# A gated-delta recurrence issued as a list of parts, with its product scalings on VectorE and its diagonal fills split over two engines

## The chip, the core and the metric

The kernel runs on one core of a Trainium2 chip. The metric is device time in microseconds (us) of one execution, lower is better. Five engines run their own instruction streams in order: TensorE (PE; its weight loads are shown as PEld), VectorE (DVE), ScalarE (ACT), GpSimd (POOL) and SyncE (SP, which issues the DMAs here). They wait for each other by semaphores.

## The reference, cut to what matters

One layer of a bidirectional backbone: a modulated norm, an input projection, two token mixers (a gated DeltaNet and a diagonal state-space model), gated merges, and a gated MLP with a 3x3 convolution. The change concerns the DeltaNet. Per head and direction, over chunks of tokens:

```python
lmat = jnp.where(strict, jnp.einsum('nbhcd,nbhsd->nbhcs', kb, k) * decay, 0.0)
sol = lax.linalg.triangular_solve(lmat, rhs, left_side=True, lower=True, unit_diagonal=True)
...
def step(state, xs):
    v_new = u_i - jnp.einsum('bhck,bhkv->bhcv', w_i, state)
    o = (jnp.einsum('bhck,bhkv->bhcv', q_i * jnp.exp(g_i)[..., None], state)
         + jnp.einsum('bhcs,bhsv->bhcv', a_i, v_new))
    state = (state * jnp.exp(g_last)[..., None]
             + jnp.einsum('bhck,bhcv->bhkv', k_i * jnp.exp(g_last - g_i)[..., None], v_new))
```

There are 4 heads of 128 columns and two directions; 1024 latent tokens follow 256 context tokens.

## The kernel before

The kernel works in chunks of 128 tokens: ten of them (two of context, eight of latents), taken forwards by direction 0 and in the mirrored order by direction 1. Step n handles one chunk of each direction, four heads at a time. Its work falls into these pieces:

- `delta_u` makes the decay matrix (the `gm` products of GpSimd, a matmul, an exponential on ScalarE, `affine_select` on GpSimd) and from it the triangular matrix `u` (VectorE, L928).
- `delta_pre` inverts it. The blocks of 32 on the diagonal are inverted in five levels (the **chain**): a matmul with `Ub` (L989), a copy by ScalarE into `Pe` (L992), a matmul with `Pe` (L995), a predicated copy and a transpose on VectorE (L974, L998). Then VectorE puts the diagonal blocks into the full matrices `Rf` and `Qf` (the **diagonal fills**, L1000 and L1001, four copies each), two rounds of corner products complete them, and a refinement step (`eh`, `el`, `dl`, `R2`; L1065 to L1086) makes the inverse `R2` exact enough. Chains of even and odd steps have their own tiles and PSUM bank (`la`, `lb`).
- `delta_step` is the recurrence: `ks` = keys times the state S (L1106); ScalarE scales it by row into `y` (L1108, four instructions); GpSimd adds `vtok` (L1109); `ty` = `R2` times y (L1113); VectorE multiplies by beta (L1115); `ds` (L1119); VectorE makes the new S (L1124). GpSimd prepares `kd` and `Sd`.
- `delta_out` makes the output: queries times S (L1138), scaled by ScalarE into `ob` (L1144, four instructions), queries times keys (L1147), and the product with y (L1152). `delta_post` norms a finished chunk.

The stage lies between the gate projections (`pz`, `pg`: plain large matmuls) and the gated linear unit (`gl`). `run` starts the chains of steps 0 and 1 ahead of the projections, so that they run beside them. The order on each engine is made by the framework's scheduler from the program's order in `delta`, one step after the other; the projections and the unit after the stage are ordered by it too. SP's queue holds the loads of `y_lo`, `w_raw` and `x` for what follows.

Of the kernel before, what the change touches and what calls it, by code (L numbers as in the profile page):

```python
# [7 lines left out]
F32 = mybir.dt.float32  # L8
# [14 lines left out]
NH = 4  # L23
# [22 lines left out]
class Zones:  # L46
# [6 lines left out]

DELTA_ZONES = {n: z for z, names in {
# [7 lines left out]
class Kernel:  # L62
    def __init__(self, tc, ins, out, stack):
        self.tc, self.nc, self.ins, self.out, self.es = tc, tc.nc, ins, out, stack
        self.dbg = {}
        self.flip = 0

# [825 lines left out]
    def delta_u(self, n, cs, tile, tag):  # L893
        nc, ps = self.nc, self.ps
        v, g_ = nc.vector, nc.gpsimd

        def b3(x):
            return x[:, :, None].to_broadcast([128, NH, 128])
# [4 lines left out]
        u = tile([128, 2 * NH, 128], F32, "u32", n)  # L903
        ats = []
        for r in range(2):
            c = cs[r]
            hs = slice(4 * r, 4 * r + 4)
            sp = bank()
            for i in range(2):
                gm = tile([128, NH, 128], F32R, "gm%d" % i, n)  # L910
                (g_).tensor_tensor(gm, (self.m_le, self.m_ge)[r][:, None, :].to_broadcast([128, NH, 128]),
                                 b3(r32(self.g_hl[i])[:, c, hs]), op=OP.mult)
                nc.tensor.matmul(sp.rearrange("p h i -> p (h i)"), lhsT=self.mr[r], rhs=gm.rearrange("p h i -> p (h i)"),
                                 start=(i == 0), stop=(i == 1))
            ei = tile([128, NH, 128], F32, "ei%d" % r, n)
# [3 lines left out]
            for out, cmp in ((es, OP.is_gt), (ei, OP.is_ge)):  # L919
                if cmp == OP.is_gt or c >= NCX:  # L920
                    g_.affine_select(out=out, in_=ei, pattern=[[0, NH], [sg, 128]], base=0, channel_multiplier=-sg,
                                     compare_op=cmp, fill=0.0)
# [7 lines left out]
            ats.append(ei)  # L930
        return u, ats

    def delta_pre(self, p, n, cs, given=None):
        nc, ps = self.nc, self.ps
        v, g_ = nc.vector, nc.gpsimd
        X = 2 * NH
        f3 = "p h i -> p (h i)"

        def m3(x, k=NH):
            return x[:, None, :].to_broadcast([128, k, 128])  # L940

        par = "ab"[n % 2]

        def bank(tag="pt"):
            return ps.tile([128, 512], F32, tag=tag, name="dps")

        lb = bank("l" + par)
        lvb = lb.rearrange("p (j x i) -> p j x i", j=2, x=X)

        def part(at, n):  # L950
            return lb[:, at:at + n * NH].rearrange("p (h i) -> p h i", h=NH)

        def grp(t):
            return t.rearrange("p (h i) -> p h i", h=NH)

# [741 lines left out]
```

## Time and profile before

| | |
|---|---|
| median of 3 runs | 1920.44 us (1917.15 to 1921.73) |
| the profiled execution | 1918.41 us |
| span of its trace | 1916.5 us |
| PE busy, share of the span | 1817.7 us, 95% |
| VectorE, ScalarE, GpSimd busy | 1346.1, 723.3, 815.9 us |
| mean granted TensorE clock | 0.975 |

The profile divides the span into 40 slices. PE shows 9 tenths or more in nearly all of them; apart from the start and the last slice only the 15th to the 19th, which are the recurrence, show 7 and 8, and the granted clock of TensorE is down to 0.8 in the 15th and 16th of them (the mark 9 stands for 0.9 or more). Busy shares say where an engine has room; what an instruction waited for is in the views of the waits and of the timeline.

### The profile page before, as it was taken

How to read it: one execution, taken by the hardware profiler on the slowest of the kernel's cores; microseconds unless marked ns; L12 is line 12 of the kernel's file. 1: busy time of each engine (PE TensorE's matmuls, PEld its weight loads, DVE VectorE, ACT ScalarE, POOL GpSimd, SP SyncE). 2: the span in 40 equal slices, each digit the busy share in tenths (PEclk: the TensorE clock that was granted, in tenths of full speed). 3: DMA queues.
4: the chain of work that ended last, by engine and by line, in shares of the span. 5: the costliest groups of instructions: out<-in, count | busy, mean ns of one | idle time of the engine just before them, and what ended most of it. 6: DMA issues, size and time to landing. Idle time of an engine off the chain costs nothing.

```text
span 1916.5 us, 27632 instructions
## 1 busy us (share of the span) xinstructions
PE 1817.7 (95%) x10874; PEld 1497.5 (78%) x10874; DVE 1346.1 (70%) x1922; ACT 723.3 (38%) x1457; POOL 815.9 (43%) x562
## 2 busy tenths in 40 slices
PE   8799999999999987888999999999999999999997
PEld 2488788787899966877778887788888888888886
DVE  8869999577666456766645245986777777767778
ACT  6423223345445466676632244322211221222222
POOL 3631322356445075554522343544425444443543
PEclk9899999999999988999999999999999999999999
DMA  8132333534414300001434332211111111111102
GB/s 337 40 91 79 90 104 89 160 103 133 143 42 117 95 2 2 2 2 45 158 127 139 110 88 72 61 55 43 46 44 55 45 47 52 46 44 43 56 22 88
DMA packets 186037, 149.27 MB, mean 78 GB/s; under 512 B 21426, under 2 KB 159282, under 8 KB 185908
## 3 DMA queue, kind: packets, MB, share of 16 engines
q1 hardware_dynamic: 184468, 142.27, 24.8%
q0 software_dynamic: 1440, 5.24, 0.7%
q8 instruction: 85, 1.39, 0.3%
q14 instruction: 44, 0.36, 0.1%
HBM read 125.99 MB, written 19.40 MB: 76 GB/s over the span
## 4 chain that ended last, share of the span: by engine, by line
PE 69%; DVE 9%; ACT 4%; DMA 3%; issue 2%; POOL 2%; SPq 0%; POOLq 0%; ACTq 0%; DVEq 0%
PE up_ps L213 25%; PE dn_ps L1438 12%; PE pw L213 5%; PE pab L213 4%; PE pj L213 3%; PE pj L430 3%; PE pz L213 2%; PE pg L213 2%; PE dps L1065 1%; DMA ada_w<-in_w_ada 1%; PE ty_ps L1113 1%; PE dps L925 1%; ACT Pe L992 1%; PE o_ps L1147 1%; PE o_ps L1152 1%
## 5 line engine op out<-in xcount | busy, mean ns | idle before, releaser
L1429 DVE SCALAR_TENSOR_TENSOR cacc<-up_ps,colC,cacc 128x945 f32<-128x945 f32 (+3 forms) x360 | 430.1, 1196 | 59.0 <-ACT cacc L1419 51.8
L205 POOL TENSOR_TENSOR w_lo<-w_raw,w_hi 128x1024 fp32r<-128x1024 f32 (+1 forms) x100 | 218.0, 2181 | 418.9 <-ACT w_hi L204 398.1
L213 PE MATMUL up_ps<-h_lo,w_hi 128*128 128x512 f32 x704 | 277.8, 395 | 0.0
L213 PE MATMUL up_ps<-h_hi,w_lo 128*128 128x512 f32 x704 | 277.8, 395 | 0.0
L213 PE MATMUL up_ps<-h_hi,w_hi 128*128 128x512 f32 x704 | 277.2, 395 | 0.5 <-DVE cacc L1429 0.5
L204 ACT CAST w_hi<-w_raw 128x1024 fp32r<-128x1024 f32 (+1 forms) x110 | 105.1, 956 | 363.5 <-PE up_ps L213 163.1
L1448 DVE TENSOR_TENSOR x<-dn_ps,x 128x512 f32<-128x512 f32 x160 | 109.5, 686 | 114.1 <-PE dn_ps L1438 113.0
L213 PEld LDWEIGHTS up_ps<-h_hi,w_hi 128*128 128x128 f32 x704 | 132.0, 188 | 31.7 <-issue 0.9
L213 PEld LDWEIGHTS up_ps<-h_hi,w_lo 128*128 128x128 f32 x704 | 132.3, 188 | 30.9
L213 PEld LDWEIGHTS up_ps<-h_lo,w_hi 128*128 128x128 f32 x704 | 132.3, 188 | 30.8
L413 POOL TENSOR_TENSOR w_lo<-w_raw,w_hi 128x1024 fp32r<-128x1024 f32 x20 | 62.5, 3125 | 187.5 <-ACT w_hi L412 186.0
L1438 PE MATMUL dn_ps<-wd_lo,g_hi 128*128 128x512 f32 x352 | 138.1, 392 | 0.0
L1438 PE MATMUL dn_ps<-wd_hi,g_lo 128*128 128x512 f32 x352 | 137.5, 391 | 0.0
L1438 PE MATMUL dn_ps<-wd_hi,g_hi 128*128 128x512 f32 x352 | 135.5, 392 | 0.1
L430 PE MATMUL pj<-hl_lo,w_hi 128*128 128x512 f32 x272 | 110.0, 405 | 4.0 <-DVE hl_lo L187 2.5
L430 PE MATMUL pj<-hl_hi,w_lo 128*128 128x512 f32 x272 | 108.8, 400 | 3.0 <-POOL w_lo L413 3.0
L430 PE MATMUL pj<-hl_hi,w_hi 128*128 128x512 f32 x272 | 108.8, 400 | 0.5 <-ACT hl_hi L184 0.5
L1252 POOL TENSOR_TENSOR g_lo<-cacc,g_hi 128x1024 fp32r<-128x1024 f32 (+1 forms) x23 | 53.3, 2318 | 92.7 <-ACT g_hi L1251 89.2
L213 PE MATMUL pj<-hl_hi,w_hi 128*128 128x512 f32 (+1 forms) x256 | 89.8, 351 | 0.0
L1482 ACT ACTIVATE cacc<-cacc 128x1024 f32<-128x1024 f32 x22 | 23.3, 1058 | 175.7 <-DVE cacc L1429 175.7
L213 PE MATMUL pj<-hl_lo,w_hi 128*128 128x512 f32 (+1 forms) x256 | 88.4, 345 | 0.0
L213 PE MATMUL pj<-hl_hi,w_lo 128*128 128x512 f32 (+1 forms) x256 | 88.2, 345 | 0.0
(522 smaller groups left out, 4422.0 us busy)
## 6 DMA issues: line engine op xcount, KB each, us to landing
w_raw<-in_w_in SPq DMA_DIRECT2D x46, 512.0 KB
w_raw<-in_w_up SPq DMA_DIRECT2D x44, 512.0 KB
ada_w<-in_w_ada SPq DMA_DIRECT2D x64, 256.0 KB
wd_raw<-in_w_down SPq DMA_DIRECT2D x22, 512.0 KB
wa<-in_w_ada SPq DMA_DIRECT2D x16, 512.0 KB
g_d<-gth SPq DMA_DIRECT2D x32, 256.0 KB
t<-g_d SPq DMA_DIRECT2D x32, 256.0 KB
w_raw<-in_w_o SPq DMA_DIRECT2D x16, 512.0 KB
```

The source lines that it names most:

```text
L204: self.rounded = nc.scalar.copy(hi[:, :kt, :m], raw[:, :kt, :m]).ins
L205: self.lowered = (eng or nc.gpsimd).tensor_sub(lo[:, :kt, :m], raw[:, :kt, :m], r32(hi[:, :kt, :m])).ins
L213: mm = nc.tensor.matmul(out, lhsT=w[a][:, k, :m], rhs=h[b][k][:, sl] if isinstance(h[b], list) else h[b][:, k, sl], start=(n == 0), stop=( ...
L413: nc.gpsimd.tensor_sub(w[1], raw, r32(w[0]))
L430: nc.tensor.matmul(ps[:, :width], lhsT=w[a][:, k], rhs=h[b][:, k, :width], start=(e == 0), stop=(e == 3 * KT - 1))
L925: nc.tensor.matmul(kp[:, h, :], lhsT=self.kT[c][:, h, :], rhs=self.kT[c][:, h, :], start=True, stop=True)
L992: nc.scalar.copy(pe[g, :, g], pp[g])
L1252: (eng or self.nc.gpsimd).tensor_sub(pair[1][sl], x, r32(pair[0][sl]))
L1429: tap[:] = [v.scalar_tensor_tensor(out=o, in0=ui[:, r0 + dy:r1 + dy, c0 + dx:c1 + dx], scalar=cw[:, t * NFT + ct:t * NFT + ct + 1], in1=o, ...
L1438: nc.tensor.matmul(out, lhsT=g[a][:, i * 128:(i + 1) * 128], rhs=w[b][:, h * 512:(h + 1) * 512], start=(first and n == 0), stop=(last and ...
L1448: v.tensor_add(x2, dn, x2)
L1482: nc.scalar.activation(ga, ga, AF.Silu)
```

## The change

A small planner (`Flow`) takes the stage's work as 15 parts (generators). Each part yields, ahead of every operation, the engine, an assumed duration, the buffers it takes and the events it needs. The planner issues the operation that could start first by its assumed clocks, corrected by a rank per part (`DELTA_RANK`, a table of numbers). The stage is issued under `manual_schedule`, so this list is the order on the engines, and no scheduler moves it. Parts are, for each direction: states, keys, refinements, outputs, posts; and for both: `gm`, `u`, `uh`/`ul`, and the chains of even and of odd steps. `delta_begin` issues, ahead of the projections' second half, the chains of steps 0 and 1 to their end and of step 2 up to the inverse of its diagonal blocks; the scheduler still places these.

Three operations change: `y` is one pass on VectorE out of PSUM (four instructions, scale and add together) in place of four on ScalarE and one on GpSimd; `ob` is one VectorE instruction in place of four on ScalarE; the `Qf` fills go to ScalarE, the `Rf` fills stay on VectorE. The refinement's `eh`, `el`, `dl` and its PSUM bank (`pt0`, `pt1`) become separate for the two directions.

```diff
+class Flow:
+    HOP = {"PE": 0.35, "DVE": 0.1, "ACT": 0.1, "POOL": 0.1}
+    BIAS = 0.3
...
+                base = max([p[2] + self.HOP[p[3]]] + [self.at[x] + 0.2 for x in chain(got, events)])
+                begin = [max(base, self.clock[e]) for e, _ in ops]
+                key = min(begin) + self.BIAS * p[0]
+                if best is None or key < best[0]:
+                    best = key, p, got, begin
...
+DELTA_RANK = (-27, 1.35, -2.3, 1.84, 2.03, 2.88, -39, 2.0, 2.57, 0.89, 2.85, -11.7, 1.85, 2.7, 1.89)
...
-            for h in range(NH):
-                nc.scalar.mul(y[:, h], kp[:, h], self.egn[:, c, 4 * r + h:4 * r + h + 1])
-            nc.gpsimd.tensor_add(y, y, self.vtok[c])
+                yield op("DVE", 1.37, (), old)
+                src = y = p.tile([128, NH, 128], F32, name="y%d" % r, bufs=2)
+                for h in range(NH):
+                    v.scalar_tensor_tensor(out=y[:, h], in0=kp[:, h], scalar=self.egn[:, c, 4 * r + h:4 * r + h + 1],
+                                           in1=self.vtok[c][:, h], op0=OP.mult, op1=OP.add)
...
-        for h in range(NH):
-            nc.scalar.mul(ob[:, h], oq[:, h], self.dec[:, 0, c, 4 * r + h:4 * r + h + 1])
+        v.tensor_mul(ob, oq, self.dec[:, 0, c, 4 * r:4 * r + 4, None].to_broadcast([128, NH, 128]))
...
-        for g in G:
-            v.tensor_copy(Rf[g, :, g], R[g])
-            v.tensor_copy(Qf[g, :, g], Q[g])
...
+        for g in G:
+            v.tensor_copy(Rf[g, :, g], R[g])
+            nc.scalar.copy(Qf[g, :, g], Q[g])
...
+        for n in range(2):
+            f.begin(self.uhl_part(p, n, self.pre[n]))
+            f.begin(self.chain_part(p, n, self.pre[n]))
+        f.free("u32")
+        f.run([(0, x) for x in self.u_two(p, 2, [o[2] for o in order])])
+        return f.begin(self.chain_part(p, 2, self.pre[2]), "inverse")
...
+            (rank[3], each(lambda n: begun if n == 2 else self.chain_part(p, n, pre[n]), ns[::2])),
+            (rank[4], each(lambda n: self.chain_part(p, n, pre[n]), ns[1::2])),
...
+                (rank[5 + 5 * r], self.state_part(p, r, order[r], pre)),
+                (rank[6 + 5 * r], self.keys_part(p, r, order[r])),
+                (rank[7 + 5 * r], each(lambda n, r=r: self.refine_part(p, n, r, pre[n]), range(NCH))),
+                (rank[8 + 5 * r], each(lambda n, r=r: self.out_part(p, n, r, cs[n][r], pre[n]), ns)),
...
+        with self.tc.manual_schedule():
+            self.flow.run(parts)
```

The order of the instructions shows what the list does. First VectorE, where the projections end and the first state product follows. Before (`Rf`, `Qf`: full matrices of a chain, `u`: the triangular matrix, here of step 2; `w_lo`: the projections' weights):

```order
L1001 COPY Qf_5812<-Qcb 32x8x32 x4
L205 TENSOR_TENSOR w_lo<-w_raw,w_hi 128x1024
L1029 CAST Rf_5588<-dps 32x4x32 x4
L205 TENSOR_TENSOR w_lo<-w_raw,w_hi 128x1024
L1052 CAST Rf_5588<-dps 64x4x64 x2
L1074 SCALAR_TENSOR_TENSOR el<-dps,eh 128x512 x2
L928 SCALAR_TENSOR_TENSOR u_6835<-dps,beta,es 128x128 x4
L1115 TENSOR_TENSOR y_6595<-ty_ps,beta 128x512
```

and now, at the same place (`Qca`, `Rca`: the even chain, here of step 2):

```order
L1196 CAST Rf_5941<-dps 64x4x64 x2
L1088 COPY_PREDICATED Rca<-lvl,dps 128x256
L1129 STREAM_TRANSPOSE Qca<-Rca 128x256
L1226 SCALAR_TENSOR_TENSOR el_6808<-dps,eh_6807 128x512
L1226 SCALAR_TENSOR_TENSOR el_6818<-dps,eh_6817 128x512
L1334 TENSOR_TENSOR ei_2_6039<-o_ps,ei_2_6039 128x512
L1088 COPY_PREDICATED Rca<-lvl,dps 128x256
L1129 STREAM_TRANSPOSE Qca<-Rca 128x256
L1334 TENSOR_TENSOR ei_2_6056<-o_ps,ei_2_6056 128x512
L1296 TENSOR_TENSOR y_6776<-ty_ps,beta 128x512
```

Step 2's `u` stood just ahead of the first state product, with its chain behind it; now two levels of that chain stand ahead of it, and the corner products of step 1 too.

Second VectorE in the middle of the stage. Before:

```order
L998 STREAM_TRANSPOSE Qca<-Rca 128x256
L1115 TENSOR_TENSOR y_7154<-ty_ps,beta 128x512
L1124 TENSOR_TENSOR S_7178<-ds_ps,Sd_7155 128x512
L1154 TENSOR_TENSOR o<-o_ps,ob 128x512
L928 SCALAR_TENSOR_TENSOR u_8089<-dps,beta,es 128x128 x4
L1115 TENSOR_TENSOR y_7182<-ty_ps,beta 128x512
L974 COPY_PREDICATED Rcb<-lvl,dps 128x256
L998 STREAM_TRANSPOSE Qcb<-Rcb 128x256
L1000 COPY Rf_5810<-Rcb 32x8x32 x4
L983 COPY Qcb<-eye 128x256
L1001 COPY Qf_5812<-Qcb 32x8x32 x4
```

and now (L1284 is the scaling into `y`, L1345 the one into `ob`):

```order
L1296 TENSOR_TENSOR y_7254<-ty_ps,beta 128x512
L1088 COPY_PREDICATED Rcb<-lvl,dps 128x256
L1129 STREAM_TRANSPOSE Qcb<-Rcb 128x256
L1284 SCALAR_TENSOR_TENSOR y_7313<-ks_ps,egn,vtok_3165 128x128 x4
L1345 TENSOR_TENSOR ob<-o_ps,dec 128x512
L1039 SCALAR_TENSOR_TENSOR u_7292<-dps,beta,es 128x128 x4
L1088 COPY_PREDICATED Rcb<-lvl,dps 128x256
L1129 STREAM_TRANSPOSE Qcb<-Rcb 128x256
L1353 TENSOR_TENSOR o<-o_ps,ob 128x512
L1311 TENSOR_TENSOR S_7388<-ds_ps,Sd_7216 128x512
L1296 TENSOR_TENSOR y_7313<-ty_ps,beta 128x512
```

The two scalings now stand between the chain's predicated copies, and the eight fills in a row are gone: four remain on VectorE per step.

Third SP, at the end of the stage. Before:

```order
L1268 DMA y_lo<-y_d 128x1024 x4
L200 DMA w_raw<-in_w_glu 128x4x128 x2
L1172 DMA sz_10317<-z_d 128x4x128
L1319 DMA t_10714<-g_d 128x512
L1319 DMA t_10715<-g_d 128x512
L1319 DMA t_10718<-g_d 128x512
L1319 DMA t_10719<-g_d 128x512
L200 DMA w_raw<-in_w_glu 128x4x128 x4
L1606 DMA x_11348<-in_x 128x1024 x3
L200 DMA w_raw<-in_w_glu 128x4x128
L1606 DMA x_11348<-in_x 128x1024 x5
L200 DMA w_raw<-in_w_glu 128x4x128
```

and now:

```order
L1372 DMA sz_10280<-z_d 128x4x128
L291 DMA w_raw<-in_w_glu 128x4x128 x2
L1563 DMA t_10677<-g_d 128x512
L1512 DMA y_lo<-y_d 128x1024 x4
L1563 DMA t_10678<-g_d 128x512
L1563 DMA t_10681<-g_d 128x512
L291 DMA w_raw<-in_w_glu 128x4x128
L1563 DMA t_10682<-g_d 128x512
L291 DMA w_raw<-in_w_glu 128x4x128 x3
L1846 DMA x_11311<-in_x 128x1024 x8
L291 DMA w_raw<-in_w_glu 128x4x128 x2
```

The loads of `y_lo`, with which the unit after the stage begins, moved behind two weight loads and one `t`; all eight loads of `x` moved ahead of that unit's last two weight loads.

## Rows read from the trace of the kernel before

**Rows 1.** Busy time of each engine by stretch, with granted clock (PEclk) and DMA.

```profile
core 0: us, PE busy (x) PEld busy (x) DVE busy (x) ACT busy (x) POOL busy (x), PEclk, DMA share, GB/s
570.00:668.00 98.00, 98.00 (x993) 95.74 (x991) 54.26 (x116) 51.39 (x120) 31.66 (x27) 1.00 0.36 103
668.00:922.00 254.00, 213.55 (x2665) 187.81 (x2663) 161.57 (x363) 173.04 (x485) 142.72 (x143) 0.91 0.06 19
668.00:768.00 100.00, 80.30 (x1004) 68.56 (x1003) 58.13 (x147) 68.59 (x178) 64.81 (x66) 0.86 0.01 3
768.00:922.00 154.00, 133.25 (x1663) 119.25 (x1662) 103.44 (x217) 104.45 (x307) 77.91 (x77) 0.93 0.09 29
828.00:888.00 60.00, 54.37 (x756) 48.97 (x755) 40.18 (x91) 48.79 (x153) 29.42 (x28) 0.97 0.04 11
```

**Rows 2.** Waits of PE, 668 to 924 us (total, times, longest).

```profile
PE ds_ps L1119 <- DVE y L1115: 6.0, 2, 3.7
PE dps L995 <- ACT Pe L992: 5.6, 5, 2.2
PE o_ps L1138 <- DVE o L1154: 4.8, 2, 4.5
PE dps L989 <- DVE Qca L998: 4.4, 2, 3.4
```

**Rows 3.** Groups of VectorE's instructions by shape, 668 to 922 us.

```profile
L928 DVE SCALAR_TENSOR_TENSOR u<-dps,beta,es 128x128 f32<-128x128 f32 x64 | 18.2, 342 | 6.5 <-PE dps L925 6.4
L1115 DVE TENSOR_TENSOR y<-ty_ps,beta 128x512 f32<-128x512 f32 x20 | 13.8, 691 | 16.6 <-PE ty_ps L1113 16.5
L1000 DVE COPY Rf<-Rcb 32x256 f16<-32x256 f16 x16 | 13.4, 835 | 0.2
...
L1001 DVE COPY Qf<-Qcb 32x256 f16<-32x256 f16 x16 | 7.1, 446 | 0.2
...
L1001 DVE COPY Qf<-Qca 32x256 f16<-32x256 f16 x16 | 5.2, 328 | 0.2
L1000 DVE COPY Rf<-Rca 32x256 f16<-32x256 f16 x16 | 3.5, 220 | 0.2
```

**Rows 4.** The same of ScalarE, 668 to 922 us.

```profile
L992 ACT CAST Pe<-dps 32x256 f16<-32x256 f32 x128 | 46.2, 361 | 9.9 <-PE dps L989 7.9
L1108 ACT ACTIVATE y<-ks_ps,egn 128x128 f32<-128x128 f32 x72 | 20.6, 370 | 12.9 <-PE ks_ps L1106 12.6
L1144 ACT ACTIVATE ob<-o_ps,dec 128x128 f32<-128x128 f32 x64 | 18.3, 376 | 10.8 <-PE o_ps L1138 10.8
```

**Rows 5.** The same of GpSimd, 668 to 922 us.

```profile
L1109 POOL TENSOR_TENSOR y<-y,vtok 128x512 f32<-128x512 f32 x18 | 23.0, 1276 | 14.2 <-ACT y L1108 14.1
```

**Rows 6.** Timeline of VectorE, 733 to 741 us (start, duration; x4 merged).

```profile
733.74 5.04 DVE L1000 COPY Rf<-Rcb 32x256 f16<-32x256 f16 x4
```

**Rows 7.** Timeline of GpSimd in the same 8 us.

```profile
733.57 2.14 POOL L965 TENSOR_TENSOR ul<-u,uh 128x1024 f16<-128x1024 f32 x1 [0.98 <-ACT uh L964]
735.66 1.04 POOL L911 TENSOR_TENSOR gm<-cm,dg_hi 128x512 fp32r<-128x512 f32 x1
...
737.66 1.04 POOL L1095 TENSOR_TENSOR kd<-ktok,dec 128x512 f32<-128x512 f32 x1
```

**Rows 8.** Timeline of VectorE, 760 to 922 us: first state product of steps 3 and 9.

```profile
767.08 0.69 DVE L1115 TENSOR_TENSOR y<-ty_ps,beta 128x512 f32<-128x512 f32 x1 [3.54 <-PE ty_ps L1113]
...
914.77 0.69 DVE L1115 TENSOR_TENSOR y<-ty_ps,beta 128x512 f32<-128x512 f32 x1 [2.20 <-PE ty_ps L1113]
```

**Rows 9.** Timeline of SP's queue, 640 to 960 us.

```profile
902.06 14.21 SPq L1268 DMA_DIRECT2D y_lo<-y_d  x4
...
953.79 0.38 SPq L200 DMA_DIRECT2D w_raw<-in_w_glu  x1
```

**Rows 10.** Timeline of ScalarE after the stage.

```profile
963.68 0.62 ACT L204 CAST w_hi<-w_raw 128x512 fp32r<-128x512 f32 x1 [4.01 <-DMA w_raw<-in_w_glu]
```

**Rows 11.** Timeline of PE after the stage.

```profile
924.15 0.50 PE L213 MATMUL gl<-y_hi,w_hi 128*128 128x512 f32 x1 [3.67 <-ACT w_hi L204]
```

More of the change, by code (lines that the diff above doesn't have):

```diff
@@ L54, with op @@
+def op(engine, us, takes=(), events=(), also=()):
+    return ((engine, us), *also), takes, events
+DELTA_RANK = (-27, 1.35, -2.3, 1.84, 2.03, 2.88, -39, 2.0, 2.57, 0.89, 2.85, -11.7, 1.85, 2.7, 1.89)
 DELTA_ZONES = {n: z for z, names in {
@@ L918, in delta_u, with keep @@
             sg = 1 if r == 0 else -1
[L919 to L922, printed above, removed]
+            def keep(out, cmp):
+                g_.affine_select(out=out, in_=ei, pattern=[[0, NH], [sg, 128]], base=0, channel_multiplier=-sg,
+                                 compare_op=cmp, fill=0.0)
+            yield op("POOL", 0.65, (), (), (("PE", 0.97),))
+            keep(es, OP.is_gt)
             kp = bank()
@@ L929, in delta_u, with delta_own @@
                                        op0=OP.mult, op1=OP.mult)
[L930 to L954, printed above, removed]
+            f.free("p1")
+            if c >= NCX:
+                yield op("POOL", 0.65)
+                keep(ei, OP.is_ge)
+            ats[r] = ei
+        f.fire("u%d" % n)
+    def delta_own(self, p):
         def own(shape, dt, name, n):
@@ L1047, in delta_pre @@
                 nc.tensor.matmul(r6[A, h, :], lhsT=P6[B, h, :], rhs=Rf[B, 4 * r + h, B], start=True, stop=True)
+        yield op("ACT", 0.76, also=(("DVE", 0.86),))
         for r in range(2):
@@ new lines, in refine_part @@
+        yield op("PE", 0.46)
+        d = bank()
+        for h in range(NH):
+            for k, t in enumerate((eh, el)):
+                mm(d[:, h, :], t[:, h, :], Rf[:, 4 * r + h, :], start=(h == 0 and k == 0))
+        yield op("ACT", 0.6)
+        nc.scalar.copy(dl, d)
+        yield op("PE", 0.44)
+        for h in range(NH):
+            mm(d[:, h, :], eh[:, h, :], dl[:, h, :])
+        mm(d.rearrange(f3), self.ident16, Rf[:, hs].rearrange(f3), stop=True)
+        yield op("ACT", 0.6, (), ("ty%d%d" % (n - 2, r),) if n >= 2 else ())
@@ L1171, in delta_post @@
             self.transpose(tp[:, h, :], o[:, h, :])
[L1172 removed]
+        yield op("DVE", 0.75)
         f = "p h t -> p (h t)"
@@ L1183, in delta @@
         order = self.delta_order()
[L1184 to L1204 removed]
+        pre = self.pre
@@ new lines, in delta, with each @@
+        ns = range(2, NCH)
+        cs = [[o[n] for o in order] for n in range(NCH)]
+        own = self.delta_own(p)
+        rank = DELTA_RANK
+        def each(part, over):
+            for n in over:
+                yield from part(n)
+        parts = [
+            (rank[0], each(lambda n: self.gm_part(n, cs[n], own), ns[1:])),
+            (rank[1], each(lambda n: self.u_part(p, n, cs[n], pre[n]), ns[1:])),
+            (rank[2], each(lambda n: self.uhl_part(p, n, pre[n]), ns)),
+            (rank[3], each(lambda n: begun if n == 2 else self.chain_part(p, n, pre[n]), ns[::2])),
+            (rank[4], each(lambda n: self.chain_part(p, n, pre[n]), ns[1::2])),
+        ]
@@ new lines, in delta @@
+        posts = [c - NCX for c in chain(*cs[NCH - 2:])]
+        for r in range(2):
+            parts += [
+                (rank[5 + 5 * r], self.state_part(p, r, order[r], pre)),
+                (rank[6 + 5 * r], self.keys_part(p, r, order[r])),
+                (rank[7 + 5 * r], each(lambda n, r=r: self.refine_part(p, n, r, pre[n]), range(NCH))),
+                (rank[8 + 5 * r], each(lambda n, r=r: self.out_part(p, n, r, cs[n][r], pre[n]), ns)),
+                (rank[9 + 5 * r], each(lambda n, r=r: self.post_part(p, cs[n][r] - NCX, z_d, ("out%d%d" % (n, r),)), ns[4:6])),
+            ]
```

404 lines of the change are left out of this document (285 added, 119 removed), and 2 rows, old and new, of the table DELTA_ZONES.

## The prediction

> **What bounds the kernel now.** I read the slices of the page first: PE is busy nearly everywhere, and only the recurrence has gaps. So I cut the middle of the span into stretches [rows 1]. From 570 to 668 us (projections, with the first chains beside them) PE is busy 98.00 of 98 us at clock 1.00: work put there makes it longer, microsecond for microsecond. From 668 to 922 us (the recurrence) PE is busy 213.55 of 254 us at a mean granted clock of 0.91. That clock is a mix of the two levels, 1.2 and 2.4 GHz, and at the lower one the same matmuls show as more busy time. So I take busy time times clock as the stage's PE work at full clock: 213.55 x 0.91 = 194 us. The **density** of the stage, work over time, is 194 / 254 = 0.77, and the 60 us that are not work (40.5 us of idle PE, some 19 us of lower clock) are all that an order can win. The first 100 us are worse, 0.803 x 0.86 = 0.69; the rest has 0.865 x 0.93 = 0.80; the best long stretch, 828 to 888 us, has 0.906 x 0.97 = 0.88.
>
> Next the waits of PE [rows 2]. No single one rules: 6.0 us for `ds` behind VectorE's y, 5.6 us behind ScalarE's `Pe`, 4.8 and 4.4 us behind VectorE. Each is a short dependence with too little other work queued between its two ends. VectorE, ScalarE and GpSimd are busy 161.57, 173.04 and 142.72 of 254 us [rows 1]: none is full, and each has stretches in which the others wait for it. One of these is plain: at 733.74 us four `Rf` fills take 5.04 us on VectorE [rows 6], where a fill takes 0.22 us in the undisturbed group [rows 3]. GpSimd runs without a gap meanwhile [rows 7], and its operations end at 735.7, 736.7, 737.7 and 738.7 us; four fills that wait for one of these ends each would be through at 738.8 us, as they are. `Qca`, which is made behind such fills in VectorE's queue, is what PE waits for up to 3.4 us [rows 2].
>
> **The change part by part.**
>
> *The state product's scaling.* 18 groups go from ScalarE (20.6 us, 72 instructions) [rows 4] and GpSimd (23.0 us) [rows 5] to VectorE. The nearest row for the new instruction is L928, the same operation on 128x128 with one operand in PSUM: 342 ns [rows 3]. So VectorE gains 72 x 0.342 = 24.6 us. On the path of one step ScalarE's four and GpSimd's one (4 x 0.370 + 1.276 = 2.8 us) become 4 x 0.342 = 1.4 us, one handover less. That is 1.4 us x 10 steps per direction, but the recurrence of one direction is not what fills the stage, so I count it in the density alone. These rows have 0.342 us on VectorE against 0.370 on ScalarE: no loss by the engine. The Trainium skill, Perfetto Trace Analysis, section Optimizing Scalar/DVE Operations, speaks against the move: it has a fixed cost per instruction of about 125 ns for VectorE on PSUM and about 51 ns for ScalarE. By that page the 72 instructions would be 72 x 0.074 = 5.3 us dearer, and the forecast, all of it exposed, 1893 us (an estimate from that page). The measured rows decide, and I leave it out.
>
> *The output's scaling.* 16 groups, 18.3 us off ScalarE [rows 4]; on VectorE one instruction each, of the form of L1115 (PSUM times a broadcast column): 16 x 0.691 = 11.1 us [rows 3].
>
> *The fills.* 32 `Qf` fills leave VectorE: 7.1 + 5.2 = 12.3 us [rows 3]. ScalarE has no such row; copies of that size out of PSUM, L992, take 361 ns [rows 4], so 32 x 0.361 = 11.6 us. It could be as little as the 0.22 us of VectorE's fill, 7 us; twice L992 would be 23 us. ScalarE, relieved of 38.9 us, hides either. The `Rf` fills stay: 16.9 us for 32 where 7.0 us would do, so about 10 us of stretching remain.
>
> Sum by engine, if the stage's work is the same: VectorE 161.6 + 24.6 + 11.1 - 12.3 = 185 us; ScalarE 173.0 - 38.9 + 11.6 = 146 us; GpSimd 142.7 - 23.0 = 120 us; PE unchanged. VectorE comes near to PE.
>
> *Work moved ahead.* Step 2's `u`, two levels of its chain and step 1's corner products now stand before the first state product, as VectorE's order shows. I bound what leaves the stage on PE by 3 to 8 us: the stage's 194 us are eight full steps, so 24 us each, and this is an eighth to a third of one. I take 5 us, and put them back on the projections, where PE has no room. They win nothing by themselves; what they win is the latency of a chain, which the first 100 us at 0.69 wait for.
>
> *The order.* This is the term that decides. The list has the two chains, both directions' states and the outputs side by side, and puts other work between the ends of the short dependences of [rows 2]; states run ahead where their inverses are ready. No row shows the new density. From below it is bounded by today's 0.77, unless a new wait comes (a rival); from above by 1.00. I take 0.87: today's order reaches 0.88 over its best 60 us [rows 1], with all pieces of the stage present, and the stage's last step, a serial chain with little left beside it, will not reach that. So the stage takes (194 - 5) / 0.87 = 217 us.
>
> *The end.* `y_lo` loads now stand behind two weight loads and one `t`, and `x` ahead of the last two weight loads. Today those loads wait on the stage's buffers for 14.21 us [rows 9], and PE idles 3.67 us ahead of the first `gl` [rows 11]; ScalarE waits 4.01 us for the last weights behind `x` [rows 10]. Bounds: 3.7 us won where the first gap goes, 9 us lost where both weights, and not only the last, come after all of `x` and twice the 4.01 us is exposed with an issue between. Queue places do not say which, so I take 0.
>
> *Small edits together.* Separate `eh`, `el`, `dl` for the directions, separate PSUM banks, other tags for the projections' `zth`: freer buffers, no instruction more; they are part of the order's term.
>
> **Sum.** 254 -> 217 + 5 = 222 us, 32 us less: 1918.4 - 32 = 1886 us against the profiled execution. The median of the runs shown is 2 us above that execution, which is inside the bounds, so I forecast **1886 us**.
>
> **The rivals.**
>
> 1. *Nearly full PE.* The list hides all but the last step's tail, density 0.95 or more: (189 / 0.95) + 5 = 204 us, 1868 us; at 1.00, 194 us, 1858 us. For it: 20 us at a stretch have run without a gap. Against: VectorE at 185 of 204 us would itself need to be nine tenths busy, in order, beside it.
>
> 2. *The chains keep the pace.* The first state product of step 3 comes at 767.08 us and that of step 9 at 914.77 us [rows 8]: 147.7 us for three more chains on each side, 49 us each. If a chain's handovers, each behind a queue, take as long as now, these 148 us stay, and only the start is won: the first 100 us at 0.69 go to 0.87, 69 / 0.87 = 79 us, less the 5 us moved and with them put back. That is 20 us at most and some 12 us where the start is only half mended: 1898 to 1906 us. For it: the chain's waits are among [rows 2]. Against: a list that puts the chain's matmuls earlier shortens its queues too.
>
> 3. *Given back.* The stage gets shorter by few us, and what it gets is lost at the end [rows 9 to 11]: 1915 to 1921 us. This also takes in the case that the assumed durations are wrong enough to make a fixed list no better than the scheduler's order.
>
> 4. *Slower: VectorE's queue holds PE.* VectorE gains 35.7 us and loses 12.3 us: 23.4 us more. The new scalings stand in its queue in front of the chain's predicated copies, and PE's chain matmuls wait for those. If the order wins nothing and every added microsecond is seen by PE, 1918.4 + 23.4 = 1942 us; at half, 1930 us. It decides from the point where VectorE, with its stretched fills, has no gap left in which to catch up, about nine tenths busy: today it has 161.57 of 254 us, then 185 of 222, 0.83, below that point. The same section of Perfetto Trace Analysis in the Trainium skill says that work belongs on ScalarE when VectorE is saturated; whether it is, its busy share in the new profile tells.
>
> That the change would not do what it says I exclude: the order shows the list's order on the engines, the scalings on VectorE and half the fills gone.
>
> **How the numbers follow.** What a measurement of this kernel can tell from no change is about 0.3%, 6 us. The forecast (density 0.83 to 0.94: 1900 to 1870 us) gets 0.56; nearly full PE 0.11; chains keep the pace 0.17; given back 0.07; slower 0.09. Faster is 0.56 + 0.11 + 0.17 = 0.84. The range of 8 in 10 reaches from 1862 us, inside the first rival, to 1910 us, past the second; outside lie the best third of rival 1 and rivals 3 and 4, 0.04 + 0.07 + 0.09 = 0.20.
>
> **What would show each step.** Right: the stretch from the last `pg` matmul to the first `gl` near 222 - 225 us, busy times clock over it near 0.87, and the gain largest in its first 100 us; VectorE near 185 us there, with the new `y` instructions at 0.34 us and `ob` at 0.69 us; ScalarE's `Qf` fills between 0.2 and 0.7 us; the projections some 5 us longer. The prediction is wrong if the waits of PE are led by one wait on VectorE of well over 10 us (rival 4), if steps 3 to 9 still take 148 us (rival 2), or if the gap ahead of `gl` grows by as much as the stage shrinks (rival 3).

## The result, and the profile after

The changed kernel takes 1886.48 us in the median of 4 runs (1885.86 to 1890.37) against 1920.72 us before: ratio 0.9833, 95% interval 0.9822 to 0.9845. That is faster by far more than the 0.3% that a measurement of this kernel can tell. The profiled execution took 1885.86 us, with a span of 1884.2 us. (In one experiment below, `a3`, the profiled execution was disturbed; its trace is not read, and its ratio is from its other runs.)

The stretches of the changed kernel, with the columns of [rows 1]; projections, the recurrence, its first 90 us, its rest, and the first 65 us of the projection behind it:

```profile
570.00:675.00 105.00, 103.52 (x1093) 100.48 (x1092) 60.39 (x124) 59.91 (x144) 34.29 (x31) 1.00 0.34 95
675.00:890.00 215.00, 191.70 (x2577) 171.37 (x2575) 169.15 (x402) 147.42 (x375) 118.21 (x120) 0.97 0.09 27
675.00:765.00 90.00, 76.79 (x998) 66.17 (x997) 64.29 (x159) 58.58 (x139) 52.45 (x54) 0.92 0.01 4
765.00:890.00 125.00, 114.91 (x1584) 105.20 (x1581) 104.86 (x245) 88.84 (x237) 65.77 (x66) 1.00 0.14 43
890.00:955.00 65.00, 64.62 (x272) 50.85 (x270) 35.09 (x38) 34.75 (x70) 26.30 (x22) 0.96 0.34 115
```

Work over time in the recurrence is 191.70 x 0.97 / 215 = 0.865, against 0.77 before [rows 1]. Of its parts the first 90 us have 0.785, the rest 0.92. Idle PE fell from 40.5 to 23.3 us; and as the granted clock rose from 0.91 to 0.97, busy time above the work at full clock fell from 19 to about 6 us. Of the 39 us by which the stretch got shorter (254 to 215 us), 17 are thus idle time, 13 are clock, and 8 are work that left it (194 to 186 us). ScalarE and GpSimd, 173 and 143 us before, have 147 and 118 us; VectorE has 169 us, 0.79 of the stretch.

To see where in the stage the time went, I use two landmarks that can be found in every kernel: the last `pg` matmul, where the projections end, and the state products on VectorE (`y<-ty_ps`, 20 of them). Here are the last `pg` group (a tile's view: counts, shortest/median/longest ns, first and last start), and the 7th and the 19th state product of the changed kernel (timeline of VectorE):

```profile
L304 PE MATMUL pg<-hl_hi,w_lo x96: 277/283/387, 634.0 to 674.5; 128*128 128x256 f32 x96
```

```profile
746.58 0.69 DVE L1296 TENSOR_TENSOR y<-ty_ps,beta 128x512 f32<-128x512 f32 x1 [0.44 <-PE ty_ps L1292]
...
879.31 0.68 DVE L1296 TENSOR_TENSOR y<-ty_ps,beta 128x512 f32<-128x512 f32 x1
```

(They are numbered by their start; in another order the same number can belong to another step, so small differences say little.) From the last `pg` to the 7th product ("start") it is 746.58 - 674.5 = 72.1 us, from the 7th to the 19th ("pace") 132.7 us. Before, the last `pg` started at 666.0 us and the same two products are those of [rows 8]: start 101.1 us, pace 147.7 us. So 29 us came from the start and 15 us from the pace. From the 19th product to the first `gl` it was 9.4 us and is 10.1 us. The whole balance: stage from last `pg` to first `gl` 258.16 to 214.93 us (-43.2), projections 94.0 to 101.0 us (+7.0), everything ahead of them +1.5, first `gl` to first `pab` (the output projections that follow) 49.5 to 50.3 us (+0.8), the rest +1.6; sum -32.3 us, which is the difference of the two spans, 1916.5 and 1884.2 us.

The waits of PE from 675 to 890 us (total, times, longest), to be read beside [rows 2]:

```profile
PE gl L304 <- ACT y_hi L1514: 4.7, 1, 4.7
PE dps L1124 <- ACT Pe L1120: 4.0, 5, 1.6
PE dps L1116 <- DVE Qcb L1129: 2.1, 1, 2.1
PE dps L1116 <- DVE Qca L1129: 1.9, 2, 1.5
```

The waits for `y` (6.0 us before, 0.4 us now) and for VectorE's `o` (4.8 us before, 0.7 us now) are no longer among the long ones. What is left is the chain of levels (`Pe`, `Qca`, `Qcb`), and one wait at the junction.

The groups that the change made or touched, VectorE and then ScalarE, 675 to 890 us, beside [rows 3, 4]:

```profile
L1284 DVE SCALAR_TENSOR_TENSOR y<-ks_ps,egn,vtok 128x128 f32<-128x128 f32 x72 | 19.9, 339 | 1.0 <-PE ks_ps L1280 1.0
...
L1345 DVE TENSOR_TENSOR ob<-o_ps,dec 128x512 f32<-128x512 f32 x16 | 10.9, 684 | 4.6 <-PE o_ps L1341 4.4
L1162 DVE COPY Rf<-Rca 32x256 f16<-32x256 f16 x16 | 7.2, 448 | 0.2
L1108 DVE COPY Qca<-eye 128x256 f16<-128x256 f16 x3 | 5.0, 1665 | 0.0
L1162 DVE COPY Rf<-Rcb 32x256 f16<-32x256 f16 x16 | 3.8, 237 | 0.2
L1108 DVE COPY Qcb<-eye 128x256 f16<-128x256 f16 x4 | 3.2, 801 | 0.0
```

```profile
L1120 ACT CAST Pe<-dps 32x256 f16<-32x256 f32 x124 | 44.9, 362 | 19.7 <-PE dps L1116 17.6
L1163 ACT COPY Qf<-Qca 32x256 f16<-32x256 f16 x16 | 6.4, 399 | 0.1
L1163 ACT COPY Qf<-Qcb 32x256 f16<-32x256 f16 x16 | 6.4, 398 | 0.1
```

(72 x 0.339 would be 24.4 us; the busy time of L1284 is 19.9 us, so neighbours overlap at their ends, and four take 1.1 us.)

### The profile page after: what moved, and what is told of

The parts are those of the page before. It is cut to its first block, busy times and chain, and to the rows that moved or that the text cites. A ratio compares the mean times of both kernels' runs of the same rounds, so it can differ in the third digit from the quotient of the medians.

```text
span 1884.2 us, 27551 instructions
## 1 busy us (share of the span) xinstructions
PE 1802.2 (96%) x10874; PEld 1488.5 (79%) x10874; DVE 1356.4 (72%) x1970; ACT 703.6 (37%) x1361; POOL 789.7 (42%) x542
## 4 chain that ended last, share of the span: by engine, by line
PE 54%; ACT 2%; DVE 2%; POOL 1%; issue 1%; POOLq 0%; ACTq 0%; DVEq 0%
PE up_ps L304 25%; PE dn_ps L1682 12%; PE pw L304 5%; PE pab L304 4%; PE gl L304 2%; PE dps L1211 1%; DVE cacc L1673 1%; PE o_ps L1341 1%; ACT Pe L1120 0%; PE o_ps L1349 0%; PE o_ps L1331 0%; PE dps L1035 0%; PE xn_ps L175 0%; PE ot_ps L175 0%; ACT fsq L1750 0%
## 5 line engine op out<-in xcount | busy, mean ns | idle before, releaser
L304 PEld LDWEIGHTS up_ps<-h_hi,w_hi 128*128 128x128 f32 x704 | 132.5, 189 | 31.7 <-issue 0.9
L304 PEld LDWEIGHTS up_ps<-h_lo,w_hi 128*128 128x128 f32 x704 | 132.7, 188 | 30.7
L1726 ACT ACTIVATE cacc<-cacc 128x1024 f32<-128x1024 f32 x22 | 23.3, 1058 | 175.7 <-DVE cacc L1673 175.7
```

The costliest lines, as they stand in the source:

```text
L304: mm = nc.tensor.matmul(out, lhsT=w[a][:, k, :m], rhs=h[b][k][:, sl] if isinstance(h[b], list) else h[b][:, k, sl], start=(n == 0), stop=( ...
L1726: nc.scalar.activation(ga, ga, AF.Silu)
```

## The experiments

The change is two things: the list, which fixes the order, and three engine moves (`y`, `ob`, `Qf` fills). My first theory was the prediction's: the order decides, and the moves give little. The first four runs try both apart. (The refinement's separate buffers and PSUM banks come with the list, and no run takes them away alone; `b2` below has them without the fixed order, and is no faster than the moves alone. Nor was `ob` undone alone.) Where I give what an edit costs against the changed kernel or another run, it is the difference of the two ratios times 1920 us; with their intervals it is good to some 4 us.

**Moves without the list** (`a1`): the kernel before, with only

```diff
-                nc.scalar.mul(y[:, h], kp[:, h], self.egn[...])
-            nc.gpsimd.tensor_add(y, y, self.vtok[c])
+                v.scalar_tensor_tensor(out=y[:, h], in0=kp[:, h], scalar=self.egn[...], in1=self.vtok[c][:, h], op0=OP.mult, op1=OP.add)
...
-            nc.scalar.mul(ob[:, h], oq[:, h], self.dec[...])
+        v.tensor_mul(ob, oq, self.dec[...].to_broadcast([128, NH, 128]))
...
-            v.tensor_copy(Qf[g, :, g], Q[g])
+            nc.scalar.copy(Qf[g, :, g], Q[g])
```

> The kernel before with the three engine moves alone: y as one VectorE operation per head, ob as one VectorE multiply, the first fills of Qf on ScalarE; the order is left to the scheduler as before. Theory (the list's order wins the time, by putting other work between the ends of the short dependences; the moves alone give little): 1908 to 1925 us, PE's density in the recurrence stage stays below 0.80 at full clock (before 0.77). Rival (the moves carry it: shorter chain around the state products, ScalarE and GpSimd relieved): 1885 to 1898 us, density at 0.83 or more.

Measured: 1900.14 us, ratio 0.9906 (0.9888 to 0.9925), some 18 us faster than before, between the two ranges. Its stage, from 667 to 907 us:

```profile
667.00:907.00 240.00, 211.80 (x2712) 185.68 (x2710) 175.76 (x420) 153.13 (x385) 123.11 (x126) 0.93 0.06 19
```

Density 211.80 x 0.93 / 240 = 0.82. So the moves alone are worth half of the gain: far more than my theory had. Its last `pg` starts at 669.0 us, its 7th and 19th state products at 758.85 and 898.25 us.

**The list without the moves, planned for the old operations** (`a2`): the changed kernel with the three edits above undone and the planner's durations to match, as here for `y`:

```diff
-                yield op("DVE", 1.37, (), old)
+                yield op("ACT", 1.48, (), old)
...
+                yield op("POOL", 1.28)
```

> The changed kernel with all three engine moves undone (y on ScalarE and GpSimd, ob on ScalarE, Qf fills on VectorE), the planner's durations set to match; the list stays. Theory (the list carries it): 1887 to 1900 us, two thirds of the gain of 34 us or more remains. Rival (the moves carry it): 1905 to 1921 us, two thirds or more of the gain is gone. In between, the two need each other.

Measured: 1923.57 us, ratio 1.0021 (1.0011 to 1.0031). All of the gain is gone; the time is even 2.6 us above the rival's range. The theory, that the list carries it, has fallen.

**One move undone at a time**, planned anew: `y` (`a3`) and the `Qf` fills (`a4`, planner's `also=(("DVE", 1.8),)`), with the same lines as above.

> The changed kernel with only y back on ScalarE and GpSimd (23 us of GpSimd and 20 of ScalarE for 20 of VectorE). Theory (other work lies between a kp bank's end and its use, so the longer chain is covered): 1887 to 1895 us, PE's waits for y under 3 us in the stage (0.4 in the changed kernel, 6.0 before). Rival (the state's path is what the steps go by): 1898 us or more, waits of PE for y back above 5 us.

Measured: 1900.88 us, ratio 0.9902 (0.9883 to 0.9921): 13 us for `y`. The rival's time; its other sign, waits of PE for `y` above 5 us, is not shown, as no trace of this run is read.

> The changed kernel with only the Qf fills back on VectorE (12 us from ScalarE to VectorE). Theory: within 4 us of the changed kernel, 1884 to 1890 us, as two engines that both stand idle a fifth of the stage take the fills alike. Rival (VectorE at 0.79 of the stage is close to the bound, so 12 us more of it, stretched by GpSimd's port, show on PE): 1892 to 1900 us, with PE's waits for Rf, Qf or Qc grown by 5 us or more.

Measured: 1900.99 us, ratio 0.9917 (0.9892 to 0.9943): 16 us for the fills by the ratios, 14.5 us by the medians (three of its four runs took 1900.0 to 1901.5 us, one 1907.8 us), 1 us past the rival's range. But its mechanism shows by less than it asked for: PE's largest wait is now

```profile
PE dps L1116 <- DVE Qca L1129: 6.8, 6, 2.3
```

against 1.9 us in the changed kernel, while the waits for `Qcb` got shorter. VectorE has 179.65 us of 230 us there, 0.78 of the stage, as full as in the changed kernel; it is not near a bound.

**The same order, old operations** (`d2`). `a2` was planned anew, so its order is another: counted in the traces, 972 of TensorE's 10,874 matmuls stand at another place than in the changed kernel. `d2` has the old operations at the planner's old places, and with them TensorE's order of the changed kernel but for 30 matmuls (among the projections, within the corner products, and at the first `gl`); the other engines keep the changed kernel's order through the stage:

```diff
                 yield op("DVE", 1.37, (), old)
...
-                    v.scalar_tensor_tensor(out=y[:, h], in0=kp[:, h], scalar=self.egn[...], in1=self.vtok[c][:, h], op0=OP.mult, op1=OP.add)
+                    nc.scalar.mul(y[:, h], kp[:, h], self.egn[...])
+                nc.gpsimd.tensor_add(y, y, self.vtok[c])
```

(and `ob` and the fills as in `a2`).

> The changed kernel with all three engine moves undone, as in a2_list_old_ops, but with the planner's durations left as they are, so that TensorE's order in the stage stays that of the changed kernel; a2 had planned anew (ratio 1.0021) and had another order in some 600 of TensorE's 10,927 rows. Theory (the longer state path and the fuller ScalarE and GpSimd cost the time whatever the order, the gain is that of the moves, which the order only lets through): 1912 to 1930 us. Rival (a2 was slow because its new order was a poor one, and a good order is worth as much as the moves): 1890 to 1903 us.

Measured: 1912.37 us, ratio 0.9972 (0.9963 to 0.9982), the theory's range at its lower end. With the order held, the moves are worth 0.9972 - 0.9833 = 1.4%, 27 us; without them the order is worth 5 us. One reserve: this order was planned for the new operations, and a part of the 27 us may be that it does not suit the old ones. The order that was planned for the old ones (`a2`) is slower still. Its stage:

```profile
674.00:915.00 241.00, 200.85 (x2587) 177.29 (x2585) 145.57 (x345) 166.66 (x473) 138.90 (x137) 0.95 0.07 20
```

Density 200.85 x 0.95 / 241 = 0.79. The waits of all engines there say what the moves do:

```profile
POOL y L1285 <- ACT y L1284: 28.5, 11, 5.5
...
DVE y L1296 <- PE ty_ps L1292: 13.4, 10, 2.4
...
PE ty_ps L1292 <- POOL y L1285: 9.8, 6, 2.8
...
PE dps L1124 <- ACT Pe L1120: 7.6, 10, 1.7
...
PE o_ps L1350 <- ACT ob L1346: 4.4, 7, 1.3
```

PE waits for GpSimd's `y`, GpSimd for ScalarE's `y`, and ScalarE, in whose queue the scalings stand among other work, is late with both. From the end of the last `ks` matmul to the first scaling of its group pass 36.8 us in the sum of the 18 groups (12.4 us before), and ScalarE is busy with something else in nearly all of it: `Pe` 10.2, `ob` 6.3, `Ub` 5.8 us, and smaller pieces. In the changed kernel PE waits 0.4 us in all for `y` and 0.3 us for this `ob`. The 7th and 19th products:

```profile
760.90 0.69 DVE L1296 TENSOR_TENSOR y<-ty_ps,beta 128x512 f32<-128x512 f32 x1 [0.44 <-PE ty_ps L1292]
...
904.90 0.69 DVE L1296 TENSOR_TENSOR y<-ty_ps,beta 128x512 f32<-128x512 f32 x1 [1.41 <-PE ty_ps L1292]
```

Its last `pg` starts at 675.0 us, so start 85.9, pace 144.0 us. Side by side, all in us; the last column is the mean time from the end of a group's last `ks` matmul to the finished `y`, queues included, over the 18 groups of a trace:

| kernel | start | pace | to `y` |
|---|---|---|---|
| before | 101.1 | 147.7 | 3.7 |
| `a1`, moves, scheduler's order | 89.8 | 139.4 | 1.4 |
| `d2`, old operations, the list's order | 85.9 | 144.0 | 4.9 |
| changed | 72.1 | 132.7 | 2.5 |

The moves win 8 to 11 us of pace, whichever the order, and 11 to 14 us of start; the order wins 15 to 18 us of start and 4 to 7 us of pace, and pays 7 us on the projections for it. The moves shorten the way to `y` by 2.3 to 2.4 us, whichever the order; the list by itself makes it 1.1 to 1.2 us longer, so what the order wins, it wins elsewhere.

**Is it GpSimd's share of `y`, or the path?** (`c2`): the scalings on ScalarE, the addition on VectorE, GpSimd spared:

```diff
-                    v.scalar_tensor_tensor(out=y[:, h], in0=kp[:, h], scalar=self.egn[...], in1=self.vtok[c][:, h], op0=OP.mult, op1=OP.add)
+                    nc.scalar.mul(y[:, h], kp[:, h], self.egn[...])
+                yield op("DVE", 0.69)
+                v.tensor_add(y, y, self.vtok[c])
```

> The changed kernel with y as four ScalarE scalings out of PSUM, and the addition of v on VectorE instead of GpSimd: GpSimd is spared its 23 us as in the changed kernel, ScalarE has its 20 us back, VectorE has less (18 additions for 72 operations). Undoing y whole costs 14 us. Theory (GpSimd's 1.28 us additions, their queue and the port they share with VectorE, were the cost): 1884 to 1890 us. Rival (ScalarE's share and the extra hand-over were it): 1896 to 1902 us. Half and half: 1891 to 1895 us.

Measured: 1900.20 us, ratio 0.9899 (0.9884 to 0.9914), the same as `a3`: it makes no difference that GpSimd is spared its additions. (It is not wholly out of it: beside GpSimd's other work six of the 18 additions on VectorE took 1.08 to 1.51 us where the others took 0.65 to 0.69, some 3.8 us in all.) The two steps of `y` in it (ScalarE, VectorE):

```profile
L1284 ACT ACTIVATE y<-ks_ps,egn 128x128 f32<-128x128 f32 x72 | 20.6, 372 | 4.8 <-PE ks_ps L1280 4.6
```

```profile
L1286 DVE TENSOR_TENSOR y<-y,vtok 128x512 f32<-128x512 f32 x18 | 16.0, 889 | 3.2 <-ACT y L1284 3.2
```

By durations that is 4 x 0.372 + 0.889 = 2.4 us and two queues in place of 4 x 0.339 = 1.4 us in one. But neighbours overlap, and four scalings take 1.1 us on either engine (20.6 / 18 and 19.9 / 18 us). What grows is the time in the queues: from the last `ks` matmul to the finished `y` it is 5.8 us in the mean, 2.5 us in the changed kernel. The rival holds: ScalarE's part and the handover. How PE comes to lose 13 us by it is not one wait. The stage, and all that PE waits for this `y` in it:

```profile
675.00:905.00 230.00, 198.34 (x2584) 175.36 (x2582) 172.04 (x351) 164.95 (x440) 119.50 (x118) 0.94 0.08 24
```

```profile
PE ty_ps L1293 <- DVE y L1286: 0.7, 1, 0.7
```

Its idle time is 31.7 us (23.3 in the changed kernel), and busy time above the work at full clock is 12 us (6). So the lateness is spread over many short waits, and about half of it shows as a lower clock.

**Is it VectorE's queue, in the fills?** (`c1`): the `Rf` fills on ScalarE too, the planner told (`also=(("ACT", 2.7),)`):

```diff
-            v.tensor_copy(Rf[g, :, g], R[g])
+            nc.scalar.copy(Rf[g, :, g], R[g])
```

> The changed kernel with the first fills of Rf on ScalarE too, so that all eight of a step stand on ScalarE one behind another; VectorE loses 32 to 64 copies, about 15 us. The runs so far price the undoing of the Qf fills at 14 us. Theory (those 14 us were VectorE's queue: fewer and unstretched copies there): 1878 to 1886 us. Rival (they were the length of the path through the fills, four in a row on two engines where eight stood in a row on one): 1893 to 1905 us, back towards the run with the Qf fills on VectorE (1901).

Measured: 1892.74 us, ratio 0.9858 (0.9841 to 0.9874), 0.3 us short of the rival's range and 5 us slower than the changed kernel, whose interval it just touches; its fastest run (1891.41 us) is above the changed kernel's slowest (1890.37 us). VectorE is lighter by 12 us than in the changed kernel and the kernel slower: with `a4`, eight fills in a row on either engine cost more than four on each, though here by little more than the noise, and although each of ScalarE's takes 397 to 400 ns and nothing stretches it. PE's wait for `Pe`, which is made in ScalarE's queue too, doubles (4.0 us in the changed kernel):

```profile
PE dps L1124 <- ACT Pe L1120: 7.8, 8, 3.1
```

**The copy of the identity** (`c3`) to ScalarE, ahead of the chain's first matmuls (planner: 2.0 us for ScalarE, 0.44 us for VectorE):

```diff
+        nc.scalar.copy(Q, self.eye)
...
-        v.tensor_copy(Q, self.eye)
```

> The changed kernel with the copy of the identity into the first Q of a chain on ScalarE, ahead of the chain's first matmuls, instead of on VectorE behind them, where copies took 0.8 and 1.7 us beside GpSimd for 0.23 alone and stood on the chain of waits twice (2.0 and 1.8 us). Theory (the stretched copies delay the chains): 1878 to 1884 us. Rival (other work lies there, the chains are not late): 1885 to 1889 us.

Measured: 1896.83 us, ratio 0.9880 (0.9865 to 0.9895): 9 us slower, outside both ranges. The copy itself did as hoped, as the tile's view shows for this kernel and then for the changed one:

```profile
L1093 ACT COPY Qcb<-eye x4: 404/404/406, 708.1 to 841.1; 128x256 f16<-128x256 f16 x4
L1093 ACT COPY Qca<-eye x3: 405/405/405, 728.5 to 816.4; 128x256 f16<-128x256 f16 x3
```

```profile
L1108 DVE COPY Qcb<-eye x4: 219/565/1855, 709.4 to 831.7; 128x256 f16<-128x256 f16 x4
L1108 DVE COPY Qca<-eye x3: 744/2098/2153, 729.9 to 814.2; 128x256 f16<-128x256 f16 x3
```

No run tells why the whole got slower. The list was planned anew (746 of TensorE's matmuls stand at another place); whether that or ScalarE's longer way to the chain's first matmuls cost the 9 us stays open. The same reserve holds for the sizes, not the signs, of `a3`, `a4`, `c1` and `c2`; only `d2` held the order.

**What in the list works.** Four runs.

> The changed kernel with all of the planner's ranks set to 0, so that the list goes by the earliest planned start alone; the operations are the same. The first four runs (moves without the list 0.9906, list without the moves 1.0021, both 0.9833) leave some 14 us to the list once the moves are made. Theory (the ranks, which let some chains go ahead of others, carry that part): 1896 to 1912 us. Rival (the early start of step 2's chain or the mere fact of a list carries it): 1884 to 1892 us.

The edit is `DELTA_RANK = (0,) * 15`. Measured: 1889.37 us, ratio 0.9847 (0.9833 to 0.9862), not to be told from the changed kernel, with 1,072 of TensorE's matmuls at another place. The ranks carry nothing that could be measured.

> The changed kernel with the same parts written in the same order, but the scheduler free to reorder them as it did before; step 2's chain stays ahead of the projections. Theory (the list's order carries its 14 us): 1896 to 1906 us, near the moves alone (1900). Rival (the early chain and the moves carry all): 1884 to 1892 us.

```diff
-        with self.tc.manual_schedule():
+        with nullcontext():
             self.flow.run(parts)
```

Measured: 1900.69 us, ratio 0.9906 (0.9891 to 0.9920): the same as the moves alone, as the theory had it. The fixed order is worth 14 us once the moves are made, and the early chain without it is worth nothing that shows. Its 7th and 19th products are at 760.50 and 894.39 us, its last `pg` at 675.6 us: pace 133.9 us, as in the changed kernel, but start 84.9 us. What the fixed order adds here lies in the start; what the early chain won there against `a1` (84.9 for 89.8 us) is paid on the projections (100.8 for 94.0 us).

> The changed kernel with step 2's u and the chain of levels put back into the recurrence stage instead of ahead of the projections; the list and its ranks stay. Theory (the gain of the list lies in the steady part): projections 5 to 7 us shorter, stage 8 to 12 us longer, 1888 to 1894 us. Rival (the stage's thin start is what the list mended, since steps 3 to 9 only went from 148 to 134 us, about what the moves give): stage 16 us or more longer, 1896 us or more.

```diff
-        f.run([(0, x) for x in self.u_two(p, 2, [o[2] for o in order])])
-        return f.begin(self.chain_part(p, 2, self.pre[2]), "inverse")
+        return None
```

(and step 2 is listed with the others). Measured: 1894.97 us, ratio 0.9877 (0.9864 to 0.9891), between the two ranges. The projections are 4.8 us shorter (96.2), the stage 12.2 us longer (227.1). Cut like the changed kernel's:

```profile
669.00:759.00 90.00, 74.34 (x960) 63.67 (x959) 63.23 (x156) 59.96 (x143) 55.60 (x58) 0.89 0.01 5
759.00:896.00 137.00, 124.63 (x1667) 112.43 (x1666) 110.62 (x259) 91.70 (x244) 68.08 (x70) 0.99 0.12 37
```

Its first 90 us have density 0.735 (0.785 in the changed kernel), the rest 0.90 (0.92): most of what is lost is at the start. So the early chain is worth 8 us inside the fixed order.

> The changed kernel with the copies of ya_hi on ScalarE issued behind the last of y_hi at the junction to the output projection, where PE waited 4.7 us for y_hi. Theory (the wait stands on ScalarE's queue order alone): the wait falls below 1.5 us, 1882 to 1884 us. Rival (the last o is late anyway, or the weights take over as in the kernel before, where the first wait of 3.7 us was for w_hi): 1885 to 1888 us, with the wait under another name.

```diff
-            nc.scalar.copy(hi, r32(lo))
+            act = nc.scalar.copy(hi, r32(lo)).ins
...
-        with self.tc.issue_after(self.rounded), self.tc.issue_after(dve):
+        with self.tc.issue_after(self.rounded), self.tc.issue_after(dve), self.tc.issue_after(act):
```

Measured: 1887.47 us, ratio 0.9841 (0.9826 to 0.9856), no difference: the rival. The junction on PE in the changed kernel, then in `b4` (timeline of PE):

```profile
889.39 1.22 PE L304 MATMUL gl<-y_hi,w_hi 128*128 128x512 f32 x2 [4.68 <-ACT y_hi L1514]
```

```profile
885.37 0.71 PE L304 MATMUL gl<-y_hi,w_hi 128*128 128x512 f32 x2 [0.88 <-DVE ob L1355]
886.82 0.50 PE L304 MATMUL gl<-y_lo,w_hi 128*128 128x512 f32 x1 [0.74 <-DVE y_lo L1515]
890.15 0.79 PE L304 MATMUL gl<-y_hi,w_lo 128*128 128x512 f32 x1 [2.83 <-POOL w_lo L296]
```

The wait for `y_hi` went, and GpSimd's `w_lo` was next. Its `w_hi` was ready at 878.8 us, but in GpSimd's queue it stands behind two additions of `o`, which end at 887.9 us. The first `gl` comes 2.2 us sooner after the last `pg`, and the stretch from it to the first `pab` is 54.5 us for 50.3 us.

None of the twelve beats the changed kernel.

## Why the prediction was right, and where its reasons were not

The time (1886 forecast, 1886.48 measured) and the direction stand; the share that its steps gave to the parts does not, and that the sum is right to the microsecond is luck.

- *The order as the term that decides.* **This step failed.** The prediction put nearly all of the gain on the order, and counted the shorter path of `y`, "1.4 us x 10 steps per direction", only "in the density alone", since "the recurrence of one direction is not what fills the stage". The order alone wins 5 us (`d2`), or nothing where it is planned anew for the old operations (`a2`); the moves alone win 18 us (`a1`), and 27 us inside the list's order. The way to `y` got 2.3 us shorter, not 1.4, since a queue was on it and not only the durations. Undoing `y` alone costs 13 us (`a3`), whether or not GpSimd is in it (`c2`). No engine is full, yet each operation on a path that goes through four in-order queues counts, and ScalarE's queue was where `y` and `ob` were late. That 13 us is near the 1.4 x 10 of one direction may be chance, since `a3` and `c2` have orders of their own.
- *The density.* 0.87 forecast, 0.865 measured. But the prediction had it from the order, and the order alone has 0.79 (`d2`), the moves alone 0.82 (`a1`): that the two together meet the number is luck in part. The reason given (what the order of before reached in its best 60 us) was a fair measure of what is left when the pieces are all at hand: the rest of the stage now has 0.92, the start 0.785, so the start is what keeps the mean down.
- *Where the gain falls.* "Largest in its first 100 us" is right: 29 of 44 us.
- *Work moved ahead, and the stage.* 5 us forecast, of 3 to 8; measured 194 - 186 = 8 us less in the stage and 7.0 us more on the projections. From the last `pg` to the first `gl` it takes 214.9 us, where the prediction's own sign was 222 to 225 us: 43 us won there for 37 forecast. The projections (2 us more than forecast), what lies ahead of them (1.5 us) and what lies behind the stage (2.4 us) take the surplus back: the misses cancel.
- *Durations.* `y` 339 ns for 342, `ob` 684 for 691: as costed. The Trainium skill, Perfetto Trace Analysis, section Optimizing Scalar/DVE Operations, has the higher fixed cost out of PSUM on VectorE. These rows are of whole instructions and do not show a fixed cost by itself; at this size VectorE is not the dearer engine in them, with 339 ns for 370 to 372 ns, and 276 ns (19.9 / 72) for 286 ns (20.6 / 72) by busy time. (The estimate that the prediction makes from that page should be 1886 + 5.3 = 1891 us, not 1893.) The `Qf` fills took 399 ns on ScalarE, 12.8 us in all, for the 11.6 us forecast.
- *Engines' sums.* ScalarE 147 for 146 and GpSimd 118 for 120 us. VectorE has 169 for 185: `y` keeps it busy for 19.9 us in place of 24.6, as its instructions overlap, which the row that the prediction took the price from shows too (64 of L928 are busy for 18.2 us, not 64 x 0.342 = 21.9 us [rows 3]); `Rf` fills that were thought to stay stretched at 16.9 us took 7.2 + 3.8 = 11.0 us, and with the chain that was moved ahead went 8 of the 64 `u` operations, 2.6 us.
- *The end.* 0 taken, of -3.7 to +9; measured +0.8 us to the first `pab` and +1.6 us behind it. `b4` shows that taking one wait away there wins nothing: the weights, late in GpSimd's queue, are next.
- *Rivals.* Chains that keep the pace: 147.7 us became 132.7. VectorE's queue holding PE: VectorE is 0.79 busy and no wait on it exceeds 2.1 us in all. Given back at the end: 2.4 us of 43. Nearly full PE: the density says no.

## What to carry to other kernels

In a recurrence over several in-order engines, none of which is full, price an operation by the path it stands on and by the queues it changes, not by the busy time it moves: two engines at four fills each beat either at eight (by 5 us and some 15 us), and `y` in one queue beat `y` in two although VectorE, the fullest helper, got it. Read such a path from the trace, from the last input to the result, as durations leave out the queues. No one path ranks the kernels, though: the way to `y` is shortest in `a1` (1.4 us), which is 14 us slower than the changed kernel (2.5 us). A fixed order and shorter paths need each other: the order was worth 5 us with long paths and 14 us with short ones. And to tell an order from the operations in it, hold the order and swap the operations; a planner that is told the new costs changes both at once.

## What the runs showed of the hardware

- The copy of 128x256 f16 on VectorE took 219 ns at best and 2,153 ns at worst, beside a GpSimd whose own operations kept their length (2.13 us for each `ul`); on ScalarE the same copy took 404 to 406 ns each time (`c3`). In the changed kernel six of the seven copies were long, and each of them ended 0.08 us after the GpSimd operation that was running when it began; the seventh, with no GpSimd operation beside it, took the 219 ns. The stretching is that of [rows 6, 7]; new is that an engine which is slower at its best was steadier, and that the kernel still did not gain by it.
- VectorE's addition of two SBUF operands of 128x512 f32 (`c2`) took 0.65 to 0.69 us when it began beside no running GpSimd operation, and otherwise ended 0.54 to 0.55 us after that operation's end: the six long ones of the 18 took 1.08 to 1.51 us. GpSimd pays as well: four times its next operation began within such an addition, and took 1.49 us in place of 1.04. One addition on VectorE, and GpSimd beside it:

```profile
734.71 1.49 DVE L1286 TENSOR_TENSOR y<-y,vtok 128x512 f32<-128x512 f32 x1
```

```profile
734.61 1.04 POOL L997 TENSOR_TENSOR gm<-cm,dg_hi 128x512 fp32r<-128x512 f32 x1
735.61 1.49 POOL L997 TENSOR_TENSOR gm<-cm,dg_lo 128x512 fp32r<-128x512 f32 x1
```

VectorE's product with one operand from PSUM took 0.65 to 0.69 us in the same run, with GpSimd beside it or not. The Trainium skill, GPSIMD Engine Reference, section Key points, has VectorE's instructions with two SBUF inputs among those that contend with GpSimd for the shared interface; these rows agree.
